# x loaded first and the conditioning summed in groups of four row blocks, in a single-core hybrid decoder layer

## Chip, cores and metric

One core of a Trainium2 chip. The metric is the device time of one launch in microseconds. Engines are called PE (TensorE), DVE (VectorE), ACT (ScalarE), POOL (GpSimd) and SP (SyncE, which issues nearly all DMAs here).

## What is computed

One decoder layer on 512 tokens of width 2048, in float32. The conditioning vector `c` gives six modulation vectors; two of them, shift and scale, act on the layer's first norm, and the input projection follows:

```python
c_act = jax.nn.silu(c)
mod = c_act @ w_ada[l] + b_ada[l]
sh_m, sc_m, gt_m, sh_f, sc_f, gt_f = jnp.split(mod[:, None, :], N_MOD, axis=-1)
h = rmsnorm(x, pre_mix_norm[l]) * (1.0 + sc_m) + sh_m
proj = h @ w_in[l]
...
y = jnp.concatenate([o_hg, o_gdn], axis=-1) @ w_out[l]
x = x + gt_m * rmsnorm(y, post_mix_norm[l])
h = rmsnorm(x, pre_ffn_norm[l]) * (1.0 + sc_f) + sh_f
y = jnp.square(jax.nn.relu(h @ w_ff1[l])) @ w_ff2[l]
x = x + gt_f * rmsnorm(y, post_ffn_norm[l])
```

Between projection and `w_out` stand two groups of eight heads, HGRN2 and Gated DeltaNet, in chunks of 64 tokens.

## The kernel before

Matrix products run on float32 values split in a rounded high part and a low rest (`wH`, `wL` of the weights, `hH`, `hL` of the activations), with three matmuls for each tile. The width 2048 is 16 row blocks (`kt`) of 128. Every projection is a sum over the 16 row blocks of `h`, and row block `kt` of `h` needs shift and scale of those 128 channels. The start stage overlaps that with the projections of the first two heads of each group (16 blocks of 128 columns): it projects row blocks as they become ready, in the pieces of `CUTS` (line 50; each entry: first row block, how many, and which of the 16 column blocks). Five column blocks keep a PSUM bank to themselves (`accs`, line 648); the other eleven are summed piece by piece into SBUF (`partial`): each piece ends in an eviction, a copy on ACT for the first and an add on DVE for later ones (lines 703 and 705).

Shift and scale are products of a vector with a matrix, made as follows. The weight tiles hold 128 partitions x 512: input channels on the partitions, and in the 512 columns some of the 16 channel rounds times the columns of a group of row blocks (`GROUPS`, line 56: row blocks 0 and 1 alone, then pairs). A slot (`SLOTS`) is a tile of scale and one of shift; there are 64 slots, and 128 tiles of 256 KB. The scale tile is accumulated on DVE (`ada_vector`, line 434, instructions at lines 438 and 440), one instruction for each round in the tile: four of 128 columns in the single groups, two of 256 in the pairs. The shift tile is scaled by ACT, also a piece for each round (line 449), and added whole by POOL (line 451), except in group 0, where DVE does it too (`NV = 1`). At the end of a group PE sums over the partitions (`column_sum`, tile `pc`), DVE finishes scale and shift (lines 845 to 847), and for each row block of the group PE transposes x (tile `pt`), DVE multiplies (line 858), and ACT and DVE, or ACT and POOL for every second block from the fifth on, make `hH` and `hL` (lines 862 to 868). Transposes and column sums share one PSUM bank.

The loads of the tiles go to 16 staging buffers (two of `NADA`, 14 that later stages own, line 760), seven slots ahead. x is loaded in eight pieces of 512 KB once four slots have been issued (`X_AT`, line 794). The norm's factors come from squares on ACT (line 633), a power on POOL (line 427) and a spread over PE. POOL also makes the masks of the later recurrences (`masks`, lines 371 to 399), one step for each group.

The order on PE and SP is written at build time: threads (`ada_thread`, `mod_thread`, `x_thread`, `start_unit`) are run against an assumed clock (`run`, line 876), on which each load is due a fixed time after the one ahead. A scheduler orders DVE, ACT and POOL.

Of the kernel before, what the change touches and what calls it, by code (L numbers as in the profile page):

```python
# [16 lines left out]
NADA = 2  # L17
# [7 lines left out]
X_AT = 4  # L25
# [5 lines left out]
NV = 1  # L31
# [18 lines left out]
CUTS = [(0, 2, 0, 16), (2, 2, 0, 16), (4, 2, 0, 8), (6, 2, 0, 8), (4, 4, 8, 16),  # L50
# [5 lines left out]
GROUPS = [(0,), (1,)] + [(k, k + 1) for k in range(2, KT, 2)]  # L56
SLOTS = [(g, j) for g, kts in enumerate(GROUPS) for j in range(4 * len(kts))]
ADA_REST = (4, 3, 2, 5)


def by_tiles(name, a):
# [3 lines left out]
    if name == "w_ada":  # L65
        w = a[0].reshape(P, KT, -1)
        out = []
        for g, j in SLOTS:
            n = len(GROUPS[g]) * P
            nr = 512 // n  # L70
            for seg in (1, 0):
                c0 = seg * D + GROUPS[g][0] * P
                out.append(w[:, nr * j : nr * (j + 1), c0 : c0 + n].reshape(P, 512))
# [162 lines left out]
def hybrid_layer_kernel(  # L236
# [311 lines left out]
    def sm(name):  # L548
        return bank("wh", name)
# [235 lines left out]

    def ada_thread():
        nl = 0
        for i, (g, j) in enumerate(SLOTS):
            w = len(GROUPS[g]) * P
            nr = 512 // w  # L790
            while nl < min(len(SLOTS), i + 1 + AHEAD):
                ada_slot(nl)
                nl += 1
                if nl == X_AT:
                    for tok in range(4):
                        for hf in range(2):
                            hs = slice(hf * 1024, (hf + 1) * 1024)
                            nc.sync.dma_start(out=xn4[:, tok, hs], in_=xf[tok * P : (tok + 1) * P, hs])
                            on_load(1.46)
                            xarr.append(dma[0])  # L800
                    tokens.add(("xload", 0))
                if nl == W_AT:
                    ws._load()
                if nl == LATE:
                    late_loads()
                if nl == W_AT2:
                    for _ in range(2):
                        ws._load()
            at, t = arrive.pop(i)
            yield max(0.0, at + (ADV if g > 0 else 1.0) - clock[0])  # L810
            if j == 0:
                sums[g] = [sp.tile([P, n], F32, tag=f"asum{n}", name=f"asum{n}_{g}", bufs=2)
                           for n in (256, 512)]
# [12 lines left out]
    def mod_thread():  # L826
        for g, kts in enumerate(GROUPS):
            w = len(kts) * P
            if g > 0:
                next(masking, None)  # L830
# [5 lines left out]
            asc, ash = sums.pop(g)  # L836
            pc = sm(f"pc{g}").rearrange("p (k n) -> p k n", n=64)
            nr = 1 if g < NV else 512 // w
            for i in range(n):
                column_sum(pc, i, asc[:, i * P : (i + 1) * P], ones[:, :64])  # L840
                for r in range(nr):
                    column_sum(pc, n + i, ash[:, r * w + i * P : r * w + (i + 1) * P], ones[:, :64],
                               r == 0, r == nr - 1)
# [960 lines left out]
```

## Time and profile before

| | |
|---|---|
| three runs, us | 2586.59, 2587.62, 2583.64 (median 2586.59) |
| profiled execution, us | 2583.66 |
| its span, us | 2581.9 |
| PE busy | 2469.1 us, 96% of the span |
| DVE, ACT, POOL busy | 73%, 43%, 40% |
| DMA, mean over the span | 136 GB/s |

The span runs from the first instruction to the last; the execution's own time has 1.8 us around it. Busy times of different engines overlap; a PE matmul is pipelined, so its duration (390 ns for 512 columns) is longer than the distance to the next one.

### The profile page before, as it was taken

The numbers are of one execution on the slowest core, as the hardware profiler recorded it, in microseconds if no ns is written. First come the engines' busy times: TensorE is split into PE (matmuls) and PEld (weight loads), VectorE is DVE, ScalarE is ACT, GpSimd is POOL, SyncE is SP. The second block draws the span as 40 slices with busy tenths as digits, with TensorE's granted clock in tenths as the row PEclk, the third lists the DMA queues.
The fourth block names the chain that finished last, engine by engine and source line by source line (L and its number), as shares of the span: only waits on it lengthen the run. The fifth ranks groups of instructions, "written<-read, shape, count | busy, mean of one in ns | idle before, by whom it ended". The sixth has DMA issues, their size and how long they took to land.

```text
span 2581.9 us, 34110 instructions
## 1 busy us (share of the span) xinstructions
PE 2469.1 (96%) x12627; PEld 2007.2 (78%) x12627; DVE 1875.9 (73%) x2709; ACT 1118.1 (43%) x1765; POOL 1032.4 (40%) x646
## 2 busy tenths in 40 slices
PE   5889999998999899999999999999999999999998
PEld 3667777777777778788788888888888888888876
DVE  7997877768586765634668776777768777677787
ACT  5553544544444452423444444444434434443333
POOL 5561344445444440000244535445354444533333
PEclk9999999999999999999999999999999999999999
DMA  8762434444545432344423332433424333232334
GB/s 320 255 203 74 128 119 147 139 148 138 160 142 164 139 115 82 130 140 155 154 98 133 104 135 95 146 123 106 142 95 139 110 127 135 94 114 82 122 116 161
DMA packets 127300, 350.64 MB, mean 136 GB/s; under 512 B 14247, under 2 KB 18713, under 8 KB 125981
## 3 DMA queue, kind: packets, MB, share of 16 engines
q1 hardware_dynamic: 126938, 348.41, 40.0%
q8 instruction: 99, 1.62, 0.3%
q14 instruction: 67, 0.55, 0.1%
q10 hardware_dynamic: 196, 0.06, 0.0%
HBM read 340.01 MB, written 8.40 MB: 135 GB/s over the span
## 4 chain that ended last, share of the span: by engine, by line
PE 67%; DVE 6%; POOL 1%; ACT 1%; issue 1%; DMA 1%; DVEq 0%; ACTq 0%; POOLq 0%
PE pf L331 27%; PE pg L331 22%; PE pj L331 9%; PE pout L331 7%; DVE wl L199 1%; DVE uc L1034 1%; PE pa L331 1%; DVE utmp L1032 1%; POOL y L1728 0%; POOL aacc L451 0%; PE p L331 0%; DVE x2r L1746 0%; DMA ada<-in_w_ada_dram 0%; DVE zkT L493 0%; PE pz L331 0%
## 5 line engine op out<-in xcount | busy, mean ns | idle before, releaser
L199 DVE TENSOR_TENSOR wl<-raw,wh 128x1024 fp32r<-128x1024 f32 x506 | 720.1, 1424 | 427.8 <-ACT wh L197 422.6
L197 ACT CAST wh<-raw 128x1024 fp32r<-128x1024 f32 x512 | 538.0, 1052 | 943.4 <-PE pf L331 285.9
L165 POOL TENSOR_TENSOR raw<-raw,raw 128x1024 f32<-128x1024 f32 x150 | 438.9, 2941 | 392.7 <-DMA raw<-in_w_ff_dram 181.6
L331 PE MATMUL pf<-h2L,wh 128*128 128x512 f32 x1024 | 399.9, 391 | 0.0
L331 PE MATMUL pf<-h2H,wh 128*128 128x512 f32 x1024 | 399.7, 390 | 0.0
L331 PE MATMUL pf<-h2H,wl 128*128 128x512 f32 x1024 | 399.6, 390 | 0.0
L451 POOL TENSOR_TENSOR aacc<-ada,aacc 128x512 f32<-128x512 f32 x180 | 268.9, 1494 | 253.5 <-ACT ada L449 242.2
L331 PE MATMUL pg<-wl,cH 128*128 128x512 f32 x840 | 327.6, 390 | 1.1 <-DVE wl L199 1.1
L331 PE MATMUL pg<-wh,cL 128*128 128x512 f32 x840 | 327.3, 390 | 0.0
L331 PE MATMUL pg<-wh,cH 128*128 128x512 f32 x840 | 327.3, 390 | 0.0
L331 PE MATMUL pj<-hH,wh 128*128 128x512 f32 x768 | 325.2, 423 | 0.0
L331 PE MATMUL pj<-hH,wl 128*128 128x512 f32 x768 | 305.0, 397 | 4.4 <-DVE wl L199 4.4
L331 PE MATMUL pj<-hL,wh 128*128 128x512 f32 x768 | 304.0, 396 | 0.0
L331 PEld LDWEIGHTS pf<-h2H,wh 128*128 128x128 f32 x1024 | 192.7, 188 | 39.7
L331 PEld LDWEIGHTS pf<-h2L,wh 128*128 128x128 f32 x1024 | 192.7, 188 | 39.6
L331 PEld LDWEIGHTS pf<-h2H,wl 128*128 128x128 f32 x1024 | 192.7, 188 | 39.6
L451 POOL TENSOR_TENSOR gacc<-ada,gacc 128x512 f32<-128x512 f32 x64 | 108.4, 1694 | 278.9 <-ACT ada L449 278.9
L1627 DVE TENSOR_TENSOR y<-pg,y 128x512 f32<-128x512 f32 x344 | 219.0, 682 | 0.0
L331 PEld LDWEIGHTS pg<-wl,cH 128*128 128x128 f32 x840 | 157.8, 188 | 35.0 <-DVE wl L199 2.3
L331 PEld LDWEIGHTS pg<-wh,cH 128*128 128x128 f32 x840 | 157.8, 188 | 32.7
L331 PEld LDWEIGHTS pg<-wh,cL 128*128 128x128 f32 x840 | 157.8, 188 | 32.5
L331 PEld LDWEIGHTS pj<-hH,wl 128*128 128x128 f32 x768 | 146.4, 191 | 39.2 <-DVE wl L199 6.5
(434 smaller groups left out, 3770.3 us busy)
## 6 DMA issues: line engine op xcount, KB each, us to landing
raw<-in_w_ff_dram SPq DMA_DIRECT2D x256, 512.0 KB, 4.0
raw<-in_w_in_dram SPq DMA_DIRECT2D x128, 512.0 KB, 3.4
ada<-in_w_ada_dram SPq DMA_DIRECT2D x256, 256.0 KB, 3.4
adas<-in_w_ada_dram SPq DMA_DIRECT2D x128, 256.0 KB, 4.4
raw<-in_w_out_dram SPq DMA_DIRECT2D x40, 512.0 KB, 3.5
xo<-in_x_dram SPq DMA_DIRECT2D x8, 512.0 KB, 9.4
xr<-in_x_dram SPq DMA_DIRECT2D x8, 512.0 KB, 6.8
x2d<-z SPq DMA_DIRECT2D x4, 1024.0 KB, 5.7
```

The source lines that it names most:

```text
L165: self.nc.gpsimd.tensor_tensor(out=out, in0=ra, in1=rb, op=op)
L197: self.cast = self.nc.scalar.copy(out=h, in_=raw).ins
L199: eng.tensor_tensor(out=lo, in0=raw, in1=h.bitcast(F32), op=ALU.subtract)
L331: nc.tensor.matmul(ps, lhsT=lhsT, rhs=rhs, start=start, stop=stop)
L451: nc.gpsimd.tensor_tensor(out=acc, in0=a, in1=acc, op=ALU.add)
L1032: nc.vector.tensor_tensor(out=tmp[:, :, :n], in0=xj, in1=uc[:, :, j : j + 1].broadcast_to([P, NCH, n]), op=ALU.mult)
L1034: nc.vector.tensor_tensor(out=uc[:, :, j + 1 :], in0=uc[:, :, j + 1 :], in1=tmp[:, :, :n], op=ALU.subtract)
L1627: nc.vector.tensor_tensor(out=dst, in0=ps, in1=dst, op=ALU.add)
```

## The change

- x is loaded ahead of all conditioning tiles.
- Row blocks 0 and 1 stay single, 2 and 3 stay a pair; from the fifth row block on groups are of four, with one round of 512 columns in a tile. One DVE instruction and one ACT activation now serve a tile of those groups. There are 64 slots and 128 tiles as before.
- Group 0's shift goes the same way as the others': ACT and POOL.
- The pieces of row blocks 4 to 7 are four blocks deep for all column blocks.
- The masks are tied to come behind the last power of the norm on POOL, two steps for each group.
- Staging has 18 buffers (`NADA = 4`). The sums take tiles of another pool, seven of them.
- A path that would sum on PE is written, but `PEG = 0` leaves it out.

```diff
-NADA = 2
+NADA = 4
...
-X_AT = 4
+PEG = 0
...
-NV = 1
...
-CUTS = [(0, 2, 0, 16), (2, 2, 0, 16), (4, 2, 0, 8), (6, 2, 0, 8), (4, 4, 8, 16),
+CUTS = [(0, 2, 0, 16), (2, 2, 0, 16), (4, 4, 0, 8), (4, 4, 8, 16),
         (8, 4, 0, 8), (12, 4, 0, 8), (8, 4, 8, 16), (12, 4, 8, 16)]
...
-GROUPS = [(0,), (1,)] + [(k, k + 1) for k in range(2, KT, 2)]
+GROUPS = [(0,), (1,), (2, 3)] + [tuple(range(k, k + 4)) for k in range(4, KT, 4)]
...
+    last_pow = []
...
-        nc.gpsimd.tensor_tensor(out=dst, in0=dst, in1=mhalf[:, :n], op=ALU.pow)
+        last_pow.append(nc.gpsimd.tensor_tensor(out=dst, in0=dst, in1=mhalf[:, :n], op=ALU.pow).ins)
...
     def ada_thread():
         nl = 0
+        x_loads()
...
-                if nl == X_AT:
-                    for tok in range(4):
...
             yield max(0.0, at + (ADV if g > 0 else 1.0) - clock[0])
-            if j == 0:
-                sums[g] = [sp.tile([P, n], F32, tag=f"asum{n}", name=f"asum{n}_{g}", bufs=2)
-                           for n in (256, 512)]
-            ada_vector(t[0], w, nr * j, nr, sums[g][0][:, :w], j == 0)
-            if g < NV:
-                ada_vector(t[1], w, nr * j, nr, sums[g][1][:, :w], j == 0)
+            if g < PEG:
...
             else:
+                if j == 0:
+                    sums[g] = [ada_pool_.tile([P, T], F32, tag="ada", bufs=LOOK + 1, name=f"asum{k}_{g}")
+                               for k in range(2)]
+                ada_vector(t[0], w, nr * j, nr, sums[g][0][:, :w], j == 0)
                 ada_pool(t[1], w, nr * j, nr, sums[g][1], j == 0)
...
             if g > 0:
-                next(masking, None)
+                with tc.issue_after(last_pow[-1]):
+                    for _ in range(2):
+                        next(masking, None)
```

Two places of the order that results. First POOL, from its first constants to its first adds of conditioning (`lmask`, `stril`: masks; `rstdx`: the norm's powers; `asum_0`, `asum_1`: sums of row blocks 0 and 1). Before:

```order
L359 MEMSET triu 128x128
L375 MEMSET lmask_87 128x64
L384 MEMSET stril 128x128
L360 AFFINE_SELECT triu<-triu 128x128
L378 MEMSET lmask_87 64x32 x2
...
L379 AFFINE_SELECT lmask_92<-lmask_92 64x32 x2
L381 AFFINE_SELECT lmask_92<-lmask_92 64x32 x2
L427 TENSOR_TENSOR rstdx<-rstdx,mhalf 128x1 x4
L451 TENSOR_TENSOR asum_1_338<-adas_1_1_221,asum_1_338 128x512
L451 TENSOR_TENSOR asum_1_338<-adas_2_1_225,asum_1_338 128x512
```

Now:

```order
L366 AFFINE_SELECT triu<-triu 128x128
L435 TENSOR_TENSOR rstdx<-rstdx,mhalf 128x1 x4
L381 MEMSET lmask_87 128x64
L390 MEMSET stril 128x128
L384 MEMSET lmask_87 64x32 x2
...
L385 AFFINE_SELECT lmask_92<-lmask_92 64x32 x2
L387 AFFINE_SELECT lmask_92<-lmask_92 64x32 x2
L459 TENSOR_TENSOR asum_0_280<-adas_1_1_203,asum_0_280 128x512
L459 TENSOR_TENSOR asum_0_280<-adas_2_1_207,asum_0_280 128x512
L459 TENSOR_TENSOR asum_0_280<-adas_3_1_211,asum_0_280 128x512
L459 TENSOR_TENSOR asum_1_353<-adas_1_1_221,asum_1_353 128x512
```

The masks stood ahead of the four powers; now they stand between the powers and the adds of row block 0's shift, which are new on this engine.

Then PE around the first conditioning of the fifth row block (`pc`: column sums of a group; `pt`: a row block of x transposed; `accg`, `acch`: accumulators; `pph`: an evicted part). Rows left out are further matmuls of the same kind. Before, where the second pair of these blocks (6 and 7) comes:

```order
L331 MATMUL pph_3072_2_1018<-hH,wl_892 128x512
L331 MATMUL accg_4096_172<-hH,wh_972 128x512
...
L331 MATMUL accg_5120_173<-hH,wh_972 128x512
...
L331 MATMUL accg_6144_174<-hH,wh_972 128x512
...
L331 MATMUL accg_7168_175<-hH,wh_972 128x512
...
L331 MATMUL pc_1063<-ones,asum_4_827 64x64 x2
L331 MATMUL pc_1063<-ones,asum_4_828 64x64 x4
...
L331 MATMUL accg_4096_172<-hH,wh_972 128x512
...
L342 MATMUL pt_1091<-ident,xo 128x128 x4
L331 MATMUL accg_5120_173<-hH,wh_972 128x512
...
L331 MATMUL accg_6144_174<-hH,wh_972 128x512
...
L342 MATMUL pt_1119<-ident,xo 128x128 x4
```

Now, where blocks 4 to 7 come together:

```order
L337 MATMUL pph_3072_2_968<-hH,wl_868 128x512
L337 MATMUL pc_998<-ones,asum_3_645 64x64 x2
L337 MATMUL pc_998<-ones,asum_3_646 64x64 x2
...
L348 MATMUL pt_1018<-ident,xo 128x128 x4
L337 MATMUL accg_4096_172<-hH,wh_926 128x512
...
L348 MATMUL pt_1051<-ident,xo 128x128 x4
L337 MATMUL accg_5120_173<-hH,wh_926 128x512
...
L337 MATMUL accg_4096_172<-hH,wh_926 128x512
...
L348 MATMUL pt_1073<-ident,xo 128x128 x4
L337 MATMUL accg_5120_173<-hH,wh_926 128x512
...
L337 MATMUL accg_4096_172<-hH,wh_926 128x512
...
L348 MATMUL pt_1089<-ident,xo 128x128 x4
```

Before, matmuls for blocks that were ready stood between one transpose and the next; now each transpose of the four stands behind the use of the block ahead of it, and nothing else stands there.

## Rows read from the trace of the kernel before

**Rows 1.** the page: busy time, share of the span and instructions of each engine.

```profile
PE 2469.1 (96%) x12627; PEld 2007.2 (78%) x12627; DVE 1875.9 (73%) x2709; ACT 1118.1 (43%) x1765; POOL 1032.4 (40%) x646
```

**Rows 2.** stretches of the start. Columns: stretch, its length, busy us and instructions of PE, PEld, DVE, ACT, POOL, granted TensorE clock as a share of full speed, DMA share, GB/s.

```profile
0.00:20.00 20.00, 3.25 (x16) 2.07 (x16) 12.17 (x59) 8.16 (x15) 14.64 (x63) 1.00 0.89 310
...
80.00:100.00 20.00, 14.29 (x55) 10.07 (x54) 18.49 (x27) 8.77 (x17) 12.03 (x8) 0.91 0.69 238
100.00:120.00 20.00, 14.91 (x84) 11.60 (x85) 19.42 (x30) 8.88 (x17) 11.11 (x7) 0.95 0.71 247
...
200.00:300.00 100.00, 99.29 (x621) 77.41 (x619) 80.91 (x172) 44.42 (x90) 12.85 (x17) 1.00 0.29 94
```

**Rows 3.** PE in order of time. Columns: start us, duration us, engine, line, operation, output<-inputs, shape, count, and in brackets the idle time before and what ended it. accg, acch: the accumulators of the first head's projections; pph, ppg: the parts that are evicted; pc: column sums; pt: x transposed.

```profile
27.43 0.79 PE L331 MATMUL accg<-hH,wh 128*128 128x512 f32 x1 [1.99 <-ACT hH L862]
...
37.01 1.33 PE L331 MATMUL pc<-ones,asum 128*64 128x64 f32 x20 [3.54 <-DVE asum L440]
...
42.79 0.80 PE L331 MATMUL accg<-hH,wh 128*128 128x512 f32 x1 [1.60 <-ACT hH L862]
...
78.22 1.18 PE L331 MATMUL pc<-ones,asum 128*64 128x64 f32 x24
...
102.38 0.39 PE L331 MATMUL accg<-hH,wh 128*128 128x512 f32 x1
...
110.09 0.60 PE L342 MATMUL pt<-ident,xo 128*128 128x128 f32 x4
...
180.51 0.60 PE L342 MATMUL pt<-ident,xo 128*128 128x128 f32 x4
...
220.23 0.39 PE L331 MATMUL acch<-hH,wh 128*128 128x512 f32 x1
...
231.11 0.39 PE L331 MATMUL ppg<-hH,wh 128*128 128x512 f32 x1
...
231.80 0.60 PE L342 MATMUL pk<-ident,kT 128*128 128x128 f32 x4
```

**Rows 4.** PE in order of time, two of its waits for evictions between 90 and 101 us. Columns as in Rows 3.

```profile
92.96 0.47 PE L331 MATMUL pph<-hH,wh 128*128 128x512 f32 x1 [1.29 <-DVE partg L705]
...
100.88 0.50 PE L331 MATMUL pph<-hH,wh 128*128 128x512 f32 x1 [1.84 <-DVE xo L705]
```

**Rows 5.** groups of instructions by line and shape, 0 to 230 us. Columns: line, engine, operation, output<-inputs, shapes, count | busy us, mean ns of one | idle time before and what ended it.

```profile
L440 DVE SCALAR_TENSOR_TENSOR asum<-adas,c,asum 128x256 f32<-128x256 f32 x105 | 88.4, 842 | 2.0
...
L451 POOL TENSOR_TENSOR asum<-adas,asum 128x512 f32<-128x512 f32 x52 | 76.9, 1481 | 45.7 <-ACT adas L449 43.5
...
L858 DVE SCALAR_TENSOR_TENSOR ht<-pt,sc,R 128x512 f32<-128x512 f32 x16 | 12.0, 748 | 6.2 <-PE pt L342 6.1
...
L440 DVE SCALAR_TENSOR_TENSOR asum<-adas,c,asum 128x128 f32<-128x128 f32 x45 | 16.9, 413 | 0.5
...
L705 DVE TENSOR_TENSOR parth<-pph,parth 128x512 f32<-128x512 f32 x13 | 8.9, 684 | 0.3 <-PE pph L331 0.3
```

**Rows 6.** DVE in order of time: one accumulation of 256 columns while POOL is idle, and one while POOL adds. Columns as in Rows 3.

```profile
64.35 0.47 DVE L440 SCALAR_TENSOR_TENSOR asum<-adas,c,asum 128x256 f32<-128x256 f32 x1
...
87.64 1.72 DVE L440 SCALAR_TENSOR_TENSOR asum<-adas,c,asum 128x256 f32<-128x256 f32 x1
```

**Rows 7.** what SP's DMA queue waited for, 0 to 210 us. Columns: queue and line waiting <- engine and line waited for: us in total, times, longest us.

```profile
SPq L778 <- POOL asum L451: 52.3, 26, 6.6
```

**Rows 8.** a stretch of 2 us, columns as in Rows 2.

```profile
18.00:20.00 2.00, 0.74 (x4) 0.45 (x3) 0.80 (x4) 1.52 (x3) 0.55 (x1) 1.00 1.04 424
```

**Rows 9.** all engines in order of time: the last square of x and what follows it. Columns as in Rows 3.

```profile
22.11 1.06 ACT L633 ACTIVATE junkx<-xo 128x1024 bf16<-128x1024 f32 x1
...
23.34 1.04 ACT L197 CAST wh<-raw 128x1024 fp32r<-128x1024 f32 x1
...
23.72 0.55 POOL L427 TENSOR_TENSOR rstdx<-rstdx,mhalf 128x1 f32<-128x1 f32 x1 [2.01 <-DVE rstdx L426]
...
24.70 1.28 ACT L449 ACTIVATE asum<-adas,c 128x128 f32<-128x128 f32 x4 [0.31 <-DMA adas<-in_w_ada_dram]
...
25.88 0.74 DVE L858 SCALAR_TENSOR_TENSOR ht<-pt,sc,R 128x512 f32<-128x512 f32 x1
```

**Rows 10.** POOL in order of time: the first and the last instruction of the masks, and its first adds of conditioning. Columns as in Rows 3.

```profile
1.85 0.15 POOL L375 MEMSET lmask<- 128x64 bf16 x1
...
15.71 0.51 POOL L381 TENSOR_SCALAR_AFFINE_SELECT lmask<-lmask 64x32 bf16<-64x32 bf16 x2
...
28.63 1.57 POOL L451 TENSOR_TENSOR asum<-adas,asum 128x512 f32<-128x512 f32 x1 [4.36 <-ACT adas L449]
...
32.39 2.77 POOL L451 TENSOR_TENSOR asum<-adas,asum 128x512 f32<-128x512 f32 x2 [2.19 <-ACT adas L449]
```

**Rows 11.** modulation of the fifth row block, DVE, ACT and POOL in order of time. Columns as in Rows 3.

```profile
83.14 0.74 DVE L858 SCALAR_TENSOR_TENSOR ht<-pt,sc,R 128x512 f32<-128x512 f32 x1
...
83.98 0.73 ACT L866 ACTIVATE ht<-ht,shm 128x512 f32<-128x512 f32 x1 [6.34 <-DVE ht L858]
84.74 0.62 ACT L867 CAST hH<-ht 128x512 fp32r<-128x512 f32 x1
...
85.43 1.28 POOL L868 TENSOR_TENSOR hL<-ht,hH 128x512 fp32r<-128x512 f32 x1 [5.47 <-ACT hH L867]
```

**Rows 12.** POOL in order of time, an add that nothing disturbs. Columns as in Rows 3.

```profile
130.24 1.28 POOL L451 TENSOR_TENSOR asum<-adas,asum 128x512 f32<-128x512 f32 x1 [4.15 <-ACT adas L449]
```

More of the change, by code (lines that the diff above doesn't have):

```diff
@@ L54, with slot_tiles @@
 IN1_COLS = [cc + h * P for h in range(2, NH) for cc in (C_GK, C_GQ, C_GV, C_HF, C_HQ, C_HI, C_GG, C_HG)]
-GROUPS = [(0,), (1,)] + [(k, k + 1) for k in range(2, KT, 2)]
+GROUPS = [(0,), (1,), (2, 3)] + [tuple(range(k, k + 4)) for k in range(4, KT, 4)]
 SLOTS = [(g, j) for g, kts in enumerate(GROUPS) for j in range(4 * len(kts))]
 ADA_REST = (4, 3, 2, 5)
+def slot_tiles(g, j):
+    if g < PEG:
+        return [(1 - j // 2, 2 * (j % 2) + k) for k in range(2)]
+    return [(1, j), (0, j)]
 def by_tiles(name, a):
@@ L70, in by_tiles @@
             nr = 512 // n
-            for seg in (1, 0):
+            for seg, jj in slot_tiles(g, j):
                 c0 = seg * D + GROUPS[g][0] * P
-                out.append(w[:, nr * j : nr * (j + 1), c0 : c0 + n].reshape(P, 512))
+                out.append(w[:, nr * jj : nr * (jj + 1), c0 : c0 + n].reshape(P, 512))
         for seg in ADA_REST:
@@ L784, in hybrid_layer_kernel, with x_loads @@
     masking = masks()
+    def x_loads():
+        for tok in range(4):
+            for hf in range(2):
+                hs = slice(hf * 1024, (hf + 1) * 1024)
+                nc.sync.dma_start(out=xn4[:, tok, hs], in_=xf[tok * P : (tok + 1) * P, hs])
+                on_load(1.46)
+                xarr.append(dma[0])
+        tokens.add(("xload", 0))
     def ada_thread():
         nl = 0
+        x_loads()
         for i, (g, j) in enumerate(SLOTS):
@@ L793, in ada_thread @@
                 nl += 1
-                if nl == X_AT:
-                    for tok in range(4):
[L796 to L801, printed above, removed]
                 if nl == W_AT:
@@ L810, in ada_thread @@
             yield max(0.0, at + (ADV if g > 0 else 1.0) - clock[0])
-            if j == 0:
-                sums[g] = [sp.tile([P, n], F32, tag=f"asum{n}", name=f"asum{n}_{g}", bufs=2)
-                           for n in (256, 512)]
-            ada_vector(t[0], w, nr * j, nr, sums[g][0][:, :w], j == 0)
-            if g < NV:
-                ada_vector(t[1], w, nr * j, nr, sums[g][1][:, :w], j == 0)
-            else:
+            if g < PEG:
+                if i == 0:
+                    sums["pe"] = sm("pcp").rearrange("p (k n) -> p k n", n=1)
+                for (seg, jj), a in zip(slot_tiles(g, j), t):
+                    for r in range(4):
+                        mm(sums["pe"][:, 2 * g + 1 - seg, :], a[:, r * P : (r + 1) * P],
+                           c2[:, 4 * jj + r : 4 * jj + r + 1], 4 * jj + r == 0, 4 * jj + r == KT - 1, cost=0.11)
+            else:
+                if j == 0:
+                    sums[g] = [ada_pool_.tile([P, T], F32, tag="ada", bufs=LOOK + 1, name=f"asum{k}_{g}")
+                               for k in range(2)]
+                ada_vector(t[0], w, nr * j, nr, sums[g][0][:, :w], j == 0)
                 ada_pool(t[1], w, nr * j, nr, sums[g][1], j == 0)
@@ L835, in mod_thread @@
             n = len(kts)
[L836 to L843, printed above, removed]
+            if g < PEG:
+                pc = sums["pe"][:, 2 * g : 2 * g + 2, :]
+            else:
+                asc, ash = sums.pop(g)
+                pc = sm(f"pc{g}").rearrange("p (k n) -> p k n", n=64)
+                nr = 512 // w
+                for i in range(n):
+                    column_sum(pc, i, asc[:, i * P : (i + 1) * P], ones[:, :64])
+                    for r in range(nr):
+                        column_sum(pc, n + i, ash[:, r * w + i * P : r * w + (i + 1) * P], ones[:, :64],
+                                   r == 0, r == nr - 1)
             ks = slice(kts[0], kts[0] + n)
```

## Prediction, made before the change was run

> **What bounds the kernel now.** I read the page's totals first: TensorE (PE) is busy 96% of the span [rows 1], so only a stretch where it is not can be worth much. I looked for that in the first 300 us, cut into stretches [rows 2]. After 200 us PE is busy 99.3 of 100 us; nothing here can make that shorter. Before 200 us it falls to 14 or 15 of 20 us, while VectorE (DVE) stands at 18.5 and 19.4 of 20. Then I read PE in order of time [rows 3]: first projection matmul at 27.43 us; second row block at 42.79; the first head's key transpose, which ends the stage for my count, at 231.80. At full clock 128x512 matmuls follow each other every 0.227 us (48 of them between 220.23 and 231.11). PE's order has 611 of them ahead of 231.80, in both kernels: 138.5 us. With some 12 us of transposes and column sums, 204.4 us hold about 54 us of waiting and half-clock work behind a lead-in of 27.4. Between 90 and 101 us PE waits for evictions, adds on DVE that free a PSUM bank, 1.3 and 1.8 us in the rows shown [rows 4]. So the stage is worth 81 us of non-work; the change reaches only that.
>
> **DVE's work.** The six pair groups from the fifth row block on hold 96 accumulations of 256 columns at 842 ns [rows 5]: 80.8 us. Now they are 48 of 512 columns. The trace has none. Lower end: 748 ns, the same operation at that width on another operand [rows 5]. Upper end: twice 842, 1684 ns. A 256-wide one takes 470 ns when undisturbed and up to 1720 ns while GpSimd (POOL) is adding [rows 6]; the mean holds 842 - 470 = 372 ns of disturbance. I take it once per instruction: 748 + 372 = 1120 ns, nearest the lower row. That is 53.8 us, 27.0 less. Row block 0's shift leaves DVE: 16 operations of 128 columns at 413 ns [rows 5], 6.6 us. Three evictions go, since blocks 4 to 7 are summed in one piece: 3 x 684 ns, 2.1 us. Together some 36 us of DVE, which is all but full there [rows 2]. This is cover, not time: it shows only where PE waits for DVE.
>
> **ScalarE (ACT)** does one activation of 512 columns for two of 256, and takes row block 0's 16 of 128. It is busy 8.8 and 8.9 of 20 us in the tight stretches [rows 2], so this costs nothing there; if it did, the adds of POOL would start later, which the walk below shows. Where ACT's own order holds it up, the walk counts it. **Staging** of 18 tiles instead of 16 lets the loader run nine slots ahead, not eight. SyncE's (SP) long waits are for POOL's adds [rows 7]; they are not PE's, so: nothing, and at most one add's time per group if that cover went. The eight issues of x pass eight of the conditioning on SP, but the DMA share is 1.04 there [rows 8]: the transfers, not the issues, are the limit.
>
> **The lead-in gets longer.** x's last square starts at 22.11 [rows 9]. By then DMA has moved 6.2 MB (310 GB/s over 20 us [rows 2]) and 0.8 more at 0.42 MB/us [rows 8]; the list up to there is 6.3 MB, so it runs about 0.7 MB ahead. With x first the list is 4.2 MB, landed when 4.9 MB have moved, 1.3 MB or 3.1 us before 20: 16.9 us. From that square to the end of POOL's last power took 22.11 to 24.27, 2.2 us [rows 9]: now 19.1. But the masks now stand between that power and the three adds of row block 0's shift. They took 1.85 to 16.22 us without a break, 14.1 us without triu's own select [rows 10]. Now 19.1 to 33.2. Three adds, 1.57 + 2.77 [rows 10]: 37.5. Column sums 0.7, three small DVE steps 0.4, and from the modulation to the first matmul 1.55 (25.88 to 27.43 [rows 9, 3]): **40.2, 12.8 later.** The conditioning tiles, landed by 24, are then long there.
>
> **The second block.** ACT makes row block 0's operand, then scales 4 + 12 pieces (1.28 for four) with a cast of 1.04 between [rows 9]: 40.1 + 1.3 + 1.0 + 3.8 = 46.2; POOL adds until 47.7. The chain from column sums to matmul took 37.01 to 42.79 [rows 3], of which 1.4 was DVE in other work; 4.5 gives **52.2: 3.4 regained, 9.4 late.** The same order up to 78.22 then stands at 87.6.
>
> **From 78.22 to 102.38.** Before, 54 matmuls with a pair's column sums and transposes took 24.2 us. Now no conditioning stands among them: 12.25 us plus 1.0 for evictions. PE reaches the fifth row block at 100.8, **11.0 regained, 1.6 early.** POOL just makes it: ACT scales the third of that group after row block 2's operand, about 76.7, then 14 adds at 1481 ns [rows 5] and a split of 2.6 end at 100.
>
> **The four blocks at once** cost. PE has nothing queued between their column sums and their use: it transposes one block, uses it for one projection, transposes the next. Column sums and small steps 2.2, transposes 0.6, modulation 0.74, ACT 0.73 + 0.62, POOL 1.28 [rows 11], handovers and last matmul 1.2: 7.4 for the first; then 4.9 (a split of DVE stands between), 5.3 (ACT and POOL again), 4.0, and 1.3 for the last projection: 22.9 us. Lower end 16.4, with no split and no half clock; upper end 30, with one more 1.12 ahead of seven DVE steps. I take 22.9, the order's own. Before, the same count of matmuls (192 to 216) took 102.38 to 110.09, 7.7: **15.2 lost, 13.6 late.**
>
> **To the last conditioning.** 219 matmuls from there: before, 110.09 to 186.3 (24 matmuls behind 180.51), 76.2 us with three more pairs' waits and DVE's evictions. Now 49.7 for matmuls, 2.1 for sums and transposes, 1.3 waiting at the next four (other matmuls cover them), 1.9 else: 55.0. **21.2 regained, 7.6 early.** The last 176 up to the key transpose took 45.5 and need 42.9 of work and 2.6 of waits: nothing. POOL's adds, behind wider DVE operations, take a little longer: their mean is 1481 against 1280 for an undisturbed one [rows 5, 12], a part of 201/470 of one DVE operation; at 748 that is 1.60, and 14 of them end 1.7 us later, 1.0 of it on PE.
>
> **Sum:** 12.8 - 3.4 - 11.0 + 15.2 - 21.2 + 1.0 = -6.6 us. The profiled execution took 2583.66 (span 2581.9 and 1.8 around it): **2577 us**. The median of the three is 2586.59, 2.9 higher; a result near 2580 would be the same forecast. A measurement tells about 0.2%, 5.2 us, from no change.
>
> **Rivals.** (1) **POOL becomes the bound, and it is slower.** Each add waits for a whole 512-wide DVE operation: 1.28 + 0.75 = 2.03 us. The 14, 12 and 13 adds that PE's three column sums wait for end 7.7, 6.6 and 7.2 later; of this 0.8 is slack at the first (100 against 100.8), 2.9 at the second (12 adds and two splits from 117.8 on end at 140.7, PE comes at 143.6), and 2.0 at the third (its last two adds stand behind a cast that PE's progress frees, and end at 177, PE comes at 178.7): 15.8, less the 1.0 counted: 2592. It decides from about 1.8 us an add. For it: disturbed DVE rows [rows 6], a single add of 1.57 [rows 10] and SP's waits [rows 7]; against it: the mean of 1.48. The Trainium skill, SBUF — State Buffer, section "SBUF: two separate sides", says that a DVE operation with two SBUF inputs and a GpSimd one that reads SBUF exclude each other for a whole instruction. By that rule wider operations on DVE mean fewer but longer lockouts of POOL, which is this rival; the trace shows lockouts of that length in single rows, not in the mean. Chance 0.16.
> (2) **The four-block burst is short.** At 16.4 us instead of 22.9: 2570. For it: the row durations alone; against it: DVE, ACT and POOL all hold accumulation steps in that stretch. Chance 0.22.
> (3) **The width saves nothing:** 1684 ns each. Between 74 and 101 us DVE then has 11 such, 18.5, with splits, evictions and operands 29 us: PE waits 2.8 there and 1 more for evictions, 2581. So the change does less than it says. For it: the mean's disturbed rows; against it: undisturbed ones. Chance 0.22.
>
> **How the numbers follow.** Forecast 0.40. From rival 2 with a lead-in 4 us shorter, 2566, to 2590, which takes in the burst's upper end (2584) and part of rival 1, lie about 8 in 10. Faster by over 0.2% comes from 0.32 of the forecast's 0.40 and all of rival 2: 0.54. Same: the rest of the forecast and rival 3, 0.30. Slower: rival 1, 0.16.
>
> **What would show it.** Right: first projection matmul at 40, second block at 52, fifth block's sums at 101, a sparse stretch of some 23 us behind them, key transpose at 225; 512-wide accumulations near 1.1 us. Wrong: a first matmul before 35 (the masks held nobody), adds on POOL over 1.8 us, or evictions that PE still waits for after 130 us.

## The result, and the profile after

The changed kernel took 2593.95 us (median of 9 runs, 2590.11 to 2596.81), the kernel before in the same series 2586.59 (9 runs): ratio 1.0029, 95% interval 1.0018 to 1.0039. It is 7.4 us slower; 2577 was forecast. The profiled execution took 2593.70 (span 2592.0).

The page's busy times after. PE lost one point of its share against [rows 1], DVE has 21 us less work, POOL 19 more:

```profile
PE 2473.5 (95%) x12591; PEld 2007.6 (77%) x12591; DVE 1854.7 (72%) x2633; ACT 1113.8 (43%) x1733; POOL 1051.6 (41%) x652
```

Stretches of the start, columns as in [rows 2]:

```profile
0.00:20.00 20.00, 4.37 (x12) 2.59 (x13) 6.38 (x37) 10.94 (x20) 4.41 (x19) 1.00 0.88 309
...
80.00:100.00 20.00, 17.31 (x63) 13.46 (x62) 15.25 (x15) 8.81 (x14) 15.41 (x9) 0.83 0.76 264
100.00:120.00 20.00, 14.48 (x77) 9.57 (x75) 14.57 (x21) 8.99 (x13) 11.83 (x9) 0.77 0.86 285
120.00:140.00 20.00, 17.74 (x53) 12.68 (x54) 11.80 (x13) 7.63 (x11) 12.12 (x8) 0.63 0.47 141
140.00:160.00 20.00, 17.57 (x105) 13.72 (x104) 19.53 (x19) 7.26 (x11) 16.88 (x10) 1.00 0.98 346
160.00:180.00 20.00, 16.24 (x76) 12.46 (x75) 18.84 (x19) 12.41 (x18) 14.72 (x10) 1.00 0.66 223
200.00:300.00 100.00, 99.71 (x625) 78.38 (x624) 77.92 (x169) 42.85 (x85) 10.32 (x15) 1.00 0.25 82
```

After 200 us PE is as full as before (99.71 against 99.29 of 100 us). Ahead of that, DVE does half as much in the first 20 us as in [rows 2] (6.38 against 12.17), has 5 to 8 us of idle time per 20 between 80 and 140, and is full from 140 to 180. PE looks busy from 120 to 140 (17.74), but on 53 instructions: the granted clock is 0.63, so most of this stretch ran at 1.2 and not at 2.4 GHz.

PE in order of time, columns as in [rows 3], at the milestones of the forecast (132.86 is the 217th matmul of 512 columns; the transpose at 110.09 in [rows 3] has 216 ahead of it):

```profile
40.45 0.79 PE L337 MATMUL accg<-hH,wh 128*128 128x512 f32 x1 [2.00 <-ACT hH L882]
...
52.39 0.80 PE L337 MATMUL accg<-hH,wh 128*128 128x512 f32 x1 [1.60 <-ACT hH L882]
...
91.00 0.80 PE L337 MATMUL pph<-hH,wh 128*128 128x512 f32 x1 [2.69 <-DVE parth L713]
...
107.26 0.34 PE L337 MATMUL pc<-ones,asum 128*64 128x64 f32 x4
109.35 1.03 PE L337 MATMUL pc<-ones,asum 128*64 128x64 f32 x28 [1.75 <-POOL asum L459]
...
132.86 0.63 PE L337 MATMUL accg<-hH,wh 128*128 128x512 f32 x1
...
155.70 0.50 PE L337 MATMUL ppg<-hH,wh 128*128 128x512 f32 x1 [1.40 <-DVE parth L713]
...
195.22 1.27 PE L337 MATMUL pc<-ones,asum 128*64 128x64 f32 x32
...
240.20 0.60 PE L348 MATMUL pk<-ident,kT 128*128 128x128 f32 x4
```

At 40.45 and 52.39 PE is where the forecast has it (40.2, 52.2). From there it falls behind the forecast: 6.5 us at the fifth block's sums (107.26 against 100.8), 9.2 at 132.86, 16.5 at the last sums (195.22 against 178.7). The key transpose is 8.4 us later than in [rows 3]; the medians differ by 7.4 and the two profiled executions by 10.0.

Groups of instructions, 0 to 230 us, columns as in [rows 5]:

```profile
L459 POOL TENSOR_TENSOR asum<-adas,asum 128x512 f32<-128x512 f32 x58 | 91.3, 1575 | 34.7 <-ACT adas L457 27.9 <-DMA adas<-in_w_ada_dram 3.9
L448 DVE SCALAR_TENSOR_TENSOR asum<-adas,c,asum 128x512 f32<-128x512 f32 x45 | 56.2, 1249 | 0.5
...
L878 DVE SCALAR_TENSOR_TENSOR ht<-pt,sc,R 128x512 f32<-128x512 f32 x16 | 12.0, 748 | 12.2 <-PE pt L348 12.0
...
L713 DVE TENSOR_TENSOR parth<-pph,parth 128x512 f32<-128x512 f32 x9 | 6.1, 683 | 2.2 <-PE pph L337 2.2
```

An accumulation of 512 columns took 1249 ns (1120 was taken, between 748 and 1684), an add on POOL 1575 (1600). So POOL's duration was right and DVE's short by a tenth. DVE was relieved of less than the forecast's 36 us, and POOL got more to do. From the start to the key transpose, before and after, columns as in [rows 2]:

```profile
0.00:231.80 231.80, 179.99 (x894) 136.59 (x895) 191.90 (x317) 116.72 (x229) 116.08 (x134) 0.93 0.66 228
```

```profile
0.00:240.20 240.20, 182.67 (x859) 136.88 (x860) 167.70 (x241) 112.68 (x198) 131.12 (x140) 0.92 0.64 221
```

DVE is 24.2 us lighter there (191.90 to 167.70), POOL 15.0 heavier (116.08 to 131.12).

### The profile page after: what moved, and what is told of

Read it like the earlier page. It is cut to its first block, busy times and chain, and to the rows that moved or that the text cites. A ratio compares the mean times of both kernels' runs of the same rounds, so it can differ in the third digit from the quotient of the medians.

```text
span 2592.0 us, 33905 instructions
## 1 busy us (share of the span) xinstructions
PE 2473.5 (95%) x12591; PEld 2007.6 (77%) x12591; DVE 1854.7 (72%) x2633; ACT 1113.8 (43%) x1733; POOL 1051.6 (41%) x652
## 4 chain that ended last, share of the span: by engine, by line
PE 68%; DVE 5%; POOL 1%; ACT 1%; issue 1%; DMA 1%; DVEq 0%; ACTq 0%; POOLq 0%
PE pf L337 27%; PE pg L337 22%; PE pj L337 9%; PE pout L337 7%; DVE wl L205 1%; PE pa L337 1%; POOL y L1748 0%; POOL aacc L459 0%; DMA ada<-in_w_ada_dram 0%; DVE uc L1054 0%; PE p L337 0%; DVE utmp L1052 0%; DVE x2r L1766 0%; DVE zkT L501 0%; PE pz L337 0%
```

## The experiments

I call lead-in what comes ahead of PE's first projection matmul; the edits that bear on it are x first, the late masks and row block 0's shift on POOL. The body is what follows; its edits are the groups and the cuts. The burst is the stretch in which PE transposes four blocks one after the other.

My theory from these rows (theory A of the expectations): the longer lead-in is lost for good. Rivals: POOL's adds alone are the pace and hide the lead-in; the burst of four transposes is what costs.

All times are medians in us; the ratio is to the kernel before in the same series (2586.59 for the change; 2586.30, 2586.62, 2585.89 and 2585.83 for the others) and is estimated together with its interval, so it can differ by 0.0005 from the quotient of the two medians. "First" is PE's first projection matmul, "key" the first head's key transpose.

| run | median | ratio, 95% interval | first | key |
|---|---|---|---|---|
| the change | 2593.95 | 1.0029 [1.0018, 1.0039] | 40.45 | 240.20 |
| e_lead | 2580.66 | 0.9972 [0.9961, 0.9984] | 28.06 | 229.44 |
| e_pairs | 2598.19 | 1.0043 [1.0030, 1.0055] | 39.72 | 243.82 |
| e_lead_pairs | 2586.59 | 1.0001 [0.9992, 1.0010] | 27.36 | 232.90 |
| e_nomasktie | 2596.02 | 1.0039 [1.0026, 1.0053] | 44.40 | 243.72 |
| e_maskend | 2597.98 | 1.0044 [1.0032, 1.0057] | 37.24 | 247.65 |
| e_xm | 2587.57 | 1.0009 [1.0000, 1.0018] | 37.23 | 236.39 |
| e_nv1 | 2582.76 | 0.9990 [0.9981, 0.9999] | 32.08 | 232.01 |
| e_cuts2 | 2588.83 | 1.0008 [1.0000, 1.0017] | 40.89 | 236.98 |
| e_lead_cuts2 | 2582.74 | 0.9981 [0.9972, 0.9990] | 28.21 | 227.35 |
| e_halves | 2599.54 | 1.0051 [1.0038, 1.0064] | 39.71 | 248.26 |
| e_halfpool | 2583.43 | 0.9988 [0.9979, 0.9997] | 40.98 | 233.70 |
| e_halfdve | 2581.18 | 0.9982 [0.9973, 0.9990] | 40.60 | 229.79 |
| e_bothhalf | 2575.98 | 0.9962 [0.9948, 0.9975] | 41.23 | 224.73 |
| e_lead_g46 | 2594.84 | 1.0030 [1.0019, 1.0042] | 27.51 | 236.61 |
| e_lead_tail1 | 2581.84 | 0.9988 [0.9979, 0.9997] | 27.13 | 228.88 |
| e_lead_tail2 | 2584.04 | 0.9994 [0.9985, 1.0003] | 26.99 | 232.41 |

### Lead-in against body

**e_lead**, the lead-in of before under the body of the change:

```diff
-        x_loads()
...
                 nl += 1
+                if nl == 4:
+                    x_loads()
...
-                with tc.issue_after(last_pow[-1]):
-                    for _ in range(2):
-                        next(masking, None)
+                for _ in range(2):
+                    next(masking, None)
...
-                ada_pool(t[1], w, nr * j, nr, sums[g][1], j == 0)
+                if g < 1:
+                    ada_vector(t[1], w, nr * j, nr, sums[g][1][:, :w], j == 0)
+                else:
+                    ada_pool(t[1], w, nr * j, nr, sums[g][1], j == 0)
...
-                nr = 512 // w
+                nr = 1 if g < 1 else 512 // w
```

> The lead-in of before with the body of the change: x loaded behind four slots, masks untied, row block 0's shift on DVE; groups of four, cuts and staging of the change stay. DVE's order up to row block 0's first matmul is again that of before. First projection matmul near 27.4 us. Theory A (the longer lead-in is lost for good): nearly all of the 13 us come back, 2581 to 2584 us. Rival B (what follows is paced by POOL's adds, DVE and the burst, so a lead-in earlier by 13 us is eaten by later waits): 2590 to 2595.

**e_pairs**, the body of before under the lead-in of the change:

```diff
-GROUPS = [(0,), (1,), (2, 3)] + [tuple(range(k, k + 4)) for k in range(4, KT, 4)]
+GROUPS = [(0,), (1,)] + [(k, k + 1) for k in range(2, KT, 2)]
...
-CUTS = [(0, 2, 0, 16), (2, 2, 0, 16), (4, 4, 0, 8), (4, 4, 8, 16),
+CUTS = [(0, 2, 0, 16), (2, 2, 0, 16), (4, 2, 0, 8), (6, 2, 0, 8), (4, 4, 8, 16),
```

> The lead-in of the change with the body of before: groups in pairs with 256 columns and the cuts of before; x first, masks behind the last power, row block 0's shift on ACT and POOL, 18 staging tiles stay. First projection matmul near 40 us. Theory A: 2586.6 plus most of 13 us, 2595 to 2599. Rival B (pairs give the lead-in back): 2585 to 2590.

**e_lead_pairs**, both edits together, which leaves the staging of the change (and two masks for each step):

> Lead-in, groups and cuts of before; of the change only the staging (18 tiles, sums in the other pool) and two masks for each step are left. If staging is worth nothing: 2585 to 2589. If the conditioning waits for staging tiles: under 2583.

The staging is worth nothing that these runs can tell (0.7 us). The lead-in costs 13.3 us under the fours (2593.95 - 2580.66) and, against e_lead_pairs and within the series, 10.9 under the pairs. The body gives 6.7 under the old lead-in (6.0 of e_lead and the 0.7 of the staging) and 4.2 under the new one (11.6 - 7.4). The two depend on each other by 2.4 us at most: theory A holds, little of the lead-in is given back, and the body gives 4 to 7 us, where the forecast's terms behind the second block add up to 16 (11.0 - 15.2 + 21.2 - 1.0).

### What holds the first matmul

**e_nomasktie**: the masks untied, as in e_lead, and nothing else.

> The change, but the masks are not tied behind the norm's last power: on POOL they stand ahead of the last three powers, as before the change, and no longer between powers and adds. Theory A (the longer lead-in is a real loss that nothing behind it gives back): first projection matmul near 27 us instead of 40.45, and most of these 13 us kept to the end: 2582 to 2586 us against the change's 2594. Rival B (the pace of POOL's conditioning adds sets when PE gets its column sums, so the lead-in was hidden): first matmul as early, but the sums of the last group stay near 195 us; within 3 us of the change.

The opposite came: later, not earlier. x comes first, so its first power stands at the head of POOL's order and the masks fall between the first power and the second. POOL, the first two powers:

```profile
8.71 0.55 POOL L435 TENSOR_TENSOR rstdx<-rstdx,mhalf 128x1 f32<-128x1 f32 x1 [6.32 <-DVE fold L730]
...
21.59 0.56 POOL L435 TENSOR_TENSOR rstdx<-rstdx,mhalf 128x1 f32<-128x1 f32 x1
```

**e_maskend**: all masks tied behind the last add of conditioning.

```diff
-            nc.gpsimd.tensor_tensor(out=acc, in0=a, in1=acc, op=ALU.add)
+            last_add.append(nc.gpsimd.tensor_tensor(out=acc, in0=a, in1=acc, op=ALU.add).ins)
...
-            if g > 0:
-                with tc.issue_after(last_pow[-1]):
-                    for _ in range(2):
-                        next(masking, None)
...
+        with tc.issue_after(last_add[-1]):
+            for _ in masking:
+                pass
         yield from decay_terms()
```

> The change, but the masks are tied behind the last add of the conditioning, so POOL makes them near 195 to 215 us, where it has nothing else. Theory A: as with the masks at the start, 2581 to 2586 us. Rival C (the masks have readers there: the first recurrence waits for them near 235 us): key transpose as early, but a new PE wait behind it, so 3 us or more slower than with the masks at the start.

Without any mask ahead of the adds the first matmul is only 3.2 us earlier. DVE in e_maskend, behind its accumulations for row block 0: 15 for row block 1 stand ahead of row block 0's small steps, and take 8.77 us, in part beside POOL's adds:

```profile
26.62 8.77 DVE L449 SCALAR_TENSOR_TENSOR asum<-adas,c,asum 128x128 f32<-128x128 f32 x15
35.31 0.15 DVE L862 TENSOR_TENSOR sc<-pc,vecT 128x1 f32<-128x1 f32 x1
```

At the other end rival C was right in its direction, but not in its mechanism: no reader of the masks waited. A split of weights on POOL (the low rest `wl` of a weight tile) stood behind them, and PE behind that split:

```profile
208.87 0.79 PE L337 MATMUL pph<-hH,wl 128*128 128x512 f32 x1 [6.88 <-POOL wl L205]
```

**e_xm**: x and the masks as in e_lead, the shift as in the change.

> x loaded behind four slots again and the masks untied; row block 0's shift stays on ACT and POOL, groups of four stay. DVE accumulates row block 0 from about 7 us on again. If starting DVE's conditioning late is what the lead-in costs, first matmul at 27 to 29 us and 2580 to 2584, as with the whole lead-in of before, or better by the 6.6 us of DVE that the shift no longer takes. If the shift on ACT and POOL is the cost: 2587 to 2592.

Half of the lead-in's 13.3 us goes, but the first matmul stays at 37.23: now row block 0's adds stand among the masks and wait for their tiles, and the powers stand behind both. POOL, the last of these adds and the first power:

```profile
20.48 1.26 POOL L459 TENSOR_TENSOR asum<-adas,asum 128x512 f32<-128x512 f32 x1
...
26.35 0.55 POOL L435 TENSOR_TENSOR rstdx<-rstdx,mhalf 128x1 f32<-128x1 f32 x1
```

**e_nv1**: the shift as in e_lead, and nothing else. x stays first, the masks stay behind the last power.

> The change, with row block 0's shift alone put back to DVE; x stays first, the masks stay behind the last power. POOL's masks then stand ahead of row block 1's adds only. DVE must do 32 accumulations of 128 columns (0.35 us) from 17.5 us on, then a split: first matmul near 33 us instead of 40.45. If the place of the shift behind the masks is what the lead-in costs: 2585 to 2588. If x first (DVE idle until 17.5 us) is: 2590 to 2594.

POOL's first adds, in the change (of row block 0) and in e_nv1 (of row block 1):

```profile
33.34 3.94 POOL L459 TENSOR_TENSOR asum<-adas,asum 128x512 f32<-128x512 f32 x3
```

```profile
36.87 4.01 POOL L459 TENSOR_TENSOR asum<-adas,asum 128x512 f32<-128x512 f32 x3
```

This one edit takes 11.2 us off the change, more than was expected, and makes it a little faster than the kernel before (0.9990, the interval just short of 1). The masks now hold only row block 1's adds (36.87), and the first matmul comes at 32.08. So with the shift on DVE, x first and late masks together cost little: 2.1 us against e_lead, which has neither, with overlapping intervals. What cost was that row block 0's shift was put on POOL, where nothing ahead of PE could cover it; with x and masks as in e_lead it still costs 6.9 us (e_xm, 2587.57 - 2580.66).

### Why the body gives 6 and not 16

**e_cuts2**: the CUTS line of e_pairs alone. **e_lead_cuts2**: the same on e_lead.

> The change, but blocks 4 to 7 of the first eight column blocks are projected in two pieces of two blocks instead of one of four (the cuts of before): 3, 9 and 9 matmuls instead of 3, 6 and 6 stand between the four transposes, and three evictions more follow. Theory A (PE is starved in the burst and DVE, ACT and POOL are held behind it): burst and what follows shorter, the column sums of the next group (157.28 us in the change) 3 to 6 us earlier per matmul, total 2588 to 2592. Rival B (POOL's pace or DVE's evictions bound): 2593 to 2597.

> The lead-in of before, groups of four, and blocks 4 to 7 in two pieces (the cuts of before). If the 5 us that the pieces gave with the change's lead-in add to what the lead-in gives: 5 us under the run with the lead-in alone, 2576 to 2581 by theory A, 2586 to 2590 by rival B.

With the lead-in of the change the pieces of two give 5.1 us. In the stretch from 120 to 140 us the clock is 0.91 instead of 0.63, and DVE is busy 19.18 us instead of 11.80:

```profile
120.00:140.00 20.00, 17.05 (x72) 13.41 (x71) 19.18 (x17) 8.62 (x13) 16.86 (x10) 0.91 0.65 204
```

With the lead-in of before the same edit gives nothing (2582.74 against 2580.66, overlapping intervals, and a key transpose 2.1 us earlier). That the burst always costs 5 us, theory A of e_cuts2, is refuted.

**e_halves**: each DVE accumulation of 512 columns as two of 256.

```diff
+        if ncol == 512:
+            cv = c2[:, r0 : r0 + 1]
+            for s in (slice(0, 256), slice(256, 512)):
...
+                    nc.vector.scalar_tensor_tensor(out=acc[:, s], in0=a[:, s], scalar=cv, in1=acc[:, s],
+                                                   op0=ALU.mult, op1=ALU.add)
+            return
```

> The change, but each accumulation of 512 columns on DVE is issued as two of 256. Tests what the width is worth and whether POOL is held by it. If the width saves DVE time that PE waits for: some 45 times (2 x 842 - 1249 = 435 ns) = 20 us of DVE more, of which a third reaches PE through evictions: 2598 to 2602. Rival D (wide operations hold POOL's adds and evictions longer, so they cost what they save): 2590 to 2595, with POOL's mean add at 1.48 instead of 1.575 us.

The groups of e_halves:

```profile
L468 POOL TENSOR_TENSOR asum<-adas,asum 128x512 f32<-128x512 f32 x58 | 84.7, 1461 | 43.4 <-ACT adas L466 34.1 <-DMA adas<-in_w_ada_dram 6.5
L449 DVE SCALAR_TENSOR_TENSOR asum<-adas,c,asum 128x256 f32<-128x256 f32 x90 | 74.6, 874 | 0.0
```

The width is worth 5.6 us (2599.54 - 2593.95), of 18.4 us more work on DVE in these instructions (74.6 - 56.2). Rival D is right that wide operations hold POOL longer (1575 against 1461 an add, 6.6 us over 58), and wrong that this eats the gain.

**e_halfpool**, **e_halfdve**, **e_bothhalf**: in the groups of four, half of POOL's adds, half of DVE's accumulations, or both are left out, and with them half of the sum. The diff is that of e_bothhalf; the other two have one half of it.

```diff
-        if not first:
+        if not first and add:
...
-                ada_vector(t[0], w, nr * j, nr, sums[g][0][:, :w], j == 0)
-                ada_pool(t[1], w, nr * j, nr, sums[g][1], j == 0)
+                if g < 3 or j % 2 == 0:
+                    ada_vector(t[0], w, nr * j, nr, sums[g][0][:, :w], j == 0)
+                ada_pool(t[1], w, nr * j, nr, sums[g][1], j == 0, add=g < 3 or j % 2 == 0)
```

> The change, with part of the sum left out: of the tiles of shift in the three groups of four, every second one is scaled by ACT but not added by POOL, 24 adds of some 1.6 us less. PE's, DVE's and ACT's work stays. If POOL paces the stage behind 78 us: PE waits for no column sum and is 6 to 10 us earlier, 2584 to 2588. If DVE's order (evictions behind wide accumulations) and the burst pace it: 0 to 3 us, 2591 to 2594.

> The change, with part of the sum left out: of the tiles of scale in the three groups of four, every second one is not accumulated on DVE, 24 operations of 1.25 us less. If DVE paces the stage: the waits for evictions at 91, 151 and 155 us go, 6 to 10 us, 2584 to 2588. If POOL does: some 3 us, from adds that DVE disturbs less, 2590 to 2592.

> The change, with both halves left out: every second tile of the groups of four is neither accumulated on DVE nor added on POOL. Alone they gave 10.5 and 12.8 us. If the two engines pace different waits, the gains add: near 2571. If they hold each other up and either half removes the same loss: 2578 to 2583.

Either half is worth more than 10 us (10.5 and 12.8), both together 18.0: neither the 23.3 of two separate losses nor one shared loss. Each alone is more than either of its expectations. Leaving out adds on POOL also makes DVE's accumulations faster, 1041 ns for the same 45 in e_halfpool, and leaving out accumulations makes POOL's adds a little faster, 1514 ns for the same 58 in e_halfdve:

```profile
L448 DVE SCALAR_TENSOR_TENSOR asum<-adas,c,asum 128x512 f32<-128x512 f32 x45 | 46.8, 1041 | 0.5
```

```profile
L459 POOL TENSOR_TENSOR asum<-adas,asum 128x512 f32<-128x512 f32 x58 | 87.8, 1514 | 35.1 <-ACT adas L457 32.1
```

Left-out work also frees staging tiles earlier. In the change, waits for loads are small: 2.2 us on DVE and 3.9 on POOL from 52 to 195 us, none on PE or ACT. So earlier loads could carry a part of these gains at most.

PE in e_bothhalf: the fifth block's sums, the last sums, the key transpose.

```profile
100.29 1.15 PE L337 MATMUL pc<-ones,asum 128*64 128x64 f32 x32
...
179.87 1.15 PE L337 MATMUL pc<-ones,asum 128*64 128x64 f32 x32
...
224.73 0.60 PE L348 MATMUL pk<-ident,kT 128*128 128x128 f32 x4
```

These are the forecast's milestones (100.8, 178.7, and 224.2 as 178.7 + 45.5) to 1.2 us. PE's own order was priced about rightly; the forecast is a kernel whose vector engines have much less to do. That it is just half of the work of the fours is chance.

What the change loses against e_bothhalf is of two kinds. PE from 52 us to the key transpose, in the change and in e_bothhalf (columns: stretch, its length, PE's busy us and instructions, granted clock, DMA share, GB/s):

```profile
52.00:240.20 188.20, 168.36 (x790) 0.91 0.59 199
```

```profile
52.00:224.73 172.73, 163.13 (x789) 0.92 0.62 218
```

Of the 15.5 us between the two lengths, 10.2 are idle time of PE (19.8 against 9.6). The other 5.2 are longer busy time for the same matmuls, at a clock of 0.91 against 0.92.

**e_lead_g46**, **e_lead_tail1**, **e_lead_tail2**: e_lead with the cuts of before and other groups.

```diff
 # e_lead_g46
+GROUPS = [(0,), (1,), (2, 3), (4, 5), (6, 7)] + [tuple(range(k, k + 4)) for k in range(8, KT, 4)]
 # e_lead_tail1
+GROUPS = [(0,), (1,), (2, 3), (4, 5), (6, 7), (8, 9, 10, 11), (12, 13), (14, 15)]
 # e_lead_tail2
+GROUPS = [(0,), (1,), (2, 3), (4, 5, 6, 7), (8, 9, 10, 11), (12, 13), (14, 15)]
```

> The lead-in of before, row blocks 4 to 7 in pairs and cuts as before, fours with 512 columns from block 8 on only. No burst of four transposes while PE has nothing else: by theory A 2575 to 2580, the best of these; by rival B 2584 to 2588.

> The lead-in of before; row blocks 4 to 7 and 12 to 15 in pairs, one group of four (8 to 11), cuts of before. With four blocks at the end PE met its last column sums with 18 matmuls of the stage less ahead and stood 12 us; in pairs the last column sums come at matmul 468, as before the change (465). If the place of the burst decides: the 9 us gained up to matmul 435 in the run with fours from block 8 on are kept, 2576 to 2580. If the vector engines' work decides: one group of four gives a third of the gain of three, 2584 to 2587.

> The lead-in of before; fours for blocks 4 to 11, pairs for 12 to 15, cuts of before. If the burst at the end is what limits: 2576 to 2580; if the work on DVE and POOL: 2581 to 2584, no better than the lead-in of before with three fours (2580.7).

e_lead_g46 is outside both of its expectations. It is 11.4 us ahead of the kernel before at its 475th matmul and 2.2 behind at its 561st: the burst has moved to the last group, where PE again has nothing between the transposes.

```profile
189.49 0.60 PE L348 MATMUL pt<-ident,xo 128*128 128x128 f32 x4
192.49 0.50 PE L337 MATMUL accg<-hH,wh 128*128 128x512 f32 x1 [2.41 <-ACT hH L890]
...
203.79 1.06 PE L348 MATMUL pt<-ident,xo 128*128 128x128 f32 x4
```

So a burst in a bad place costs 13 us (2594.84 - 2581.84: e_lead_tail1 differs in the last four row blocks alone). But in e_lead_tail1 the time is e_lead's again, between its two expectations. PE waits 2.40 and 1.96 us for DVE's sums of the late pairs and 2.67 for a small step of DVE's, and of the 6.4 us by which it leads the kernel before at its 466th matmul 2.9 are left at the key transpose. e_lead_tail2 (2584.04) is no better than e_lead either, as expected where the work of DVE and POOL decides. I read this as that work being paid at the end; no run here separates it from the order of the late blocks.

## Why the prediction was wrong, step by step

- **The lead-in: right in time, wrong in what it rests on.** 40.2 was forecast, 40.45 measured, and the 3.4 us regained at the second block came as well (13.0 late, then 9.6); little of them was kept. Against e_lead the change is 12.4 us late at the first matmul, 10.8 at the key transpose, and 13.3 by the medians. The text put the delay on the masks between powers and adds. They end when it said (33.2; the first adds start at 33.34), but without them the first matmul comes only 3.2 us earlier, held by DVE's order then (e_maskend). The edit that exposes PE to the masks, the shift's move to POOL, alone decides the sign (e_nv1). The text counted that edit's delay in the lead-in, booked it as 6.6 us of relief on DVE as well, and did not ask what the change is worth without it.
- **"This is cover, not time": the step that failed.** The forecast took DVE 36 us lighter, let PE run through its order and added 1.0 us of waits from the second group to the fifth block's sums. DVE was 24 us lighter, and PE came to these sums 6.5 us later than forecast (107.26 against 100.8; 0.2 of it from the lead-in). The eviction that PE waited for at 91.00 came 2.69 us late, behind a split and a wide accumulation, and 13 matmuls behind it went at half clock (0.43 us apart instead of 0.227, 2.6 us in all; the granted clock is 0.83 from 80 to 100 us). Of the 11.0 us "regained", 4.7 came. 2.1 of the 2.69 us are the time by which POOL's adds lengthened the two operations ahead of the eviction (rows below).
- **The four-block burst: 22.9 was forecast.** From 107.26 to 132.86 it took 25.6, 1.75 of it POOL's (17.9 lost, 15.2 forecast); the mechanism holds, and the size nearly. Left out was what it does to the others: DVE is busy 11.8 of 20 us from 120 to 140, and full in the 40 us after that.
- **"To the last conditioning": 55.0 forecast, 62.4 measured** (132.86 to 195.22), so 13.9 regained and not 21.2. DVE is at 19.5 and 18.8 of 20 us there, POOL at 16.9 and 14.7. PE's waits there come to 6.8 us, all for DVE; 1.3 was counted as waiting and 1.9 as "else". They are evictions (1.02, 1.40, 1.30), a modulation (1.64) and splits (0.82, 0.60). The forecast named waits for evictions after 130 us as a sign of being wrong.
- **The sum, by the trace:** 13.0 - 3.4 - 4.7 + 17.9 - 13.9 - 0.5 = +8.4 at the key transpose, against -6.6. Of the 15.0 us between them, 13.6 are in the two terms "regained" (11.0 and 21.2), both for waits that lighter DVE work was to take away.
- **Rival 1 gave 2592, near the result, but that is chance: its mechanism did not decide.** It wanted adds over 1.8 us; they took 1.575, and only one of the three column sums waited for POOL. Yet the coupling it rests on is there, and the work of both engines is what bounds the body (e_bothhalf). It was priced for POOL alone, as PE's wait for sums. It works on both engines, and in the rows shown it reaches PE through DVE's evictions (2.69 at 91.00, 1.40 at 155.70).
- **Rivals 2 and 3** are excluded: the burst is not short (25.6), and the width saves (1249 ns and not 1684; e_halves).

What PE waited for between 132.9 and 195.3 us in the change (columns: who waits <- for whom: us in total, times, longest):

```profile
PE ppg L337 <- DVE parth L713: 2.4, 2, 1.4
PE pt L348 <- DVE ht L878: 1.6, 1, 1.6
PE pph L337 <- DVE xo L713: 1.3, 1, 1.3
```

What stood on DVE ahead of the eviction that PE waited for at 91.00, the adds of POOL beside it, and a split on DVE with POOL idle:

```profile
86.36 2.32 DVE L205 TENSOR_TENSOR wl<-raw,wh 128x1024 fp32r<-128x1024 f32 x1
88.59 1.74 DVE L448 SCALAR_TENSOR_TENSOR asum<-adas,c,asum 128x512 f32<-128x512 f32 x1
```

```profile
82.53 8.93 POOL L459 TENSOR_TENSOR asum<-adas,asum 128x512 f32<-128x512 f32 x5 [0.65 <-ACT adas L457]
```

```profile
118.27 1.22 DVE L205 TENSOR_TENSOR wl<-raw,wh 128x1024 fp32r<-128x1024 f32 x1
```

The split took 1.10 us more than with POOL idle (2.32 against 1.22), the accumulation 1.00 more (1.74 against 0.74, next rows).

That DVE and POOL lengthen each other is seen where both have work queued. An undisturbed accumulation takes 0.74 us, an undisturbed add 1.28 [rows 12], together 2.02. In the change, an undisturbed accumulation on DVE, then one beside an add of POOL's with that add, then an eviction on DVE, which reads PSUM, with the eight adds in whose midst it stands:

```profile
112.60 0.74 DVE L448 SCALAR_TENSOR_TENSOR asum<-adas,c,asum 128x512 f32<-128x512 f32 x1
```

```profile
181.97 1.67 DVE L448 SCALAR_TENSOR_TENSOR asum<-adas,c,asum 128x512 f32<-128x512 f32 x1
```

```profile
181.34 1.74 POOL L459 TENSOR_TENSOR asum<-adas,asum 128x512 f32<-128x512 f32 x1
```

```profile
183.55 0.68 DVE L713 TENSOR_TENSOR xo<-pph,xo 128x512 f32<-128x512 f32 x1
```

```profile
181.34 14.06 POOL L459 TENSOR_TENSOR asum<-adas,asum 128x512 f32<-128x512 f32 x8
```

The accumulation takes 0.93 us longer than alone, the add 0.46. From the start of the add to the end of the accumulation (181.34 to 183.64) are 2.30 us, not less than the 2.02 of the two in turn. The Trainium skill, SBUF — State Buffer, section "SBUF: two separate sides", says that of a DVE instruction with two SBUF inputs and a GpSimd instruction that reads SBUF the one that starts first has the shared port pair for the whole instruction, and the other is blocked. By these rows the trace agrees. It follows that work moved between DVE and POOL, or made wider on one, frees less than its own duration as long as both have work queued.

The row of 1.72 us in [rows 6], which the forecast took for an accumulation beside an add, stands mostly beside a split on POOL (until 89.07), in the kernel before:

```profile
86.67 2.40 POOL L199 TENSOR_TENSOR wl<-raw,wh 128x1024 fp32r<-128x1024 f32 x1
```

So splits on POOL can hold DVE up as adds do.

What stays open: how much of the idle time that e_bothhalf saves PE comes from less work on DVE and POOL and how much from their lengthening each other less; the runs change both at once. Also why the two-block pieces help under one lead-in and not under the other.

The best version that computes the whole layer is by its median e_lead (2580.66): fours, staging and cuts of the change, lead-in of before. It beats the kernel before by 6.0 us and the change by 13.3; e_lead_tail1, e_lead_cuts2 and e_nv1 are within 2.1 us of it, with overlapping intervals.

## What to carry to other kernels

Before work is taken off an engine and called cover, add up what two engines that take turns owe together in the stretch, and ask which of its consumers stands behind it in order. A small operation on the path to the first matmul may not be moved to an engine that has a long block of its own ahead, however idle that engine looks on average. Undo a bundled change edit by edit: here one of six edits, taken back, undid more than the whole loss.

## What the runs showed of the hardware that was not expected

- Accumulations with all operands in SBUF vary with POOL's load, from 1041 ns (e_halfpool) to 1249 (the change) as means of 45. DVE operations of the same width that read PSUM don't: evictions took 683 ns and the modulation 748 in the change, 684 and 748 before [rows 5], and the eviction at 183.55 took 0.68 us in the midst of eight adds of POOL's.
- After a wait of PE the granted clock can stay low while PE is busy again. Behind the wait of 2.69 us that ended at 91.00, 13 matmuls with no wait between them went 0.43 us apart; from 120 to 140 us the clock was 0.63 with PE busy for 17.74 of 20.
